# gMLP's v projection by seven products of halves, with its weight sums made on GpSimd in an earlier stage

## Chip, core and metric

One core of a Trainium2 chip runs one program. The metric is the time of one execution in device microseconds (us); the time before is the median of three runs.

## What is computed

The reference runs two transformer blocks over 512 tokens of width 1024, in float32. The change touches the gMLP branch of the first block:

```python
h = rms_norm(x, g_pre_mix)
z = h @ w_in                                  # u, v, q, kv, ... are column ranges of z
y_a = gmlp_mixer(gelu(u), gelu(v), ...)       # u * (W_s LayerNorm(v) + b), in chunks of 128 tokens
merged = g0 * (y_a @ w_br_a) + g1 * (y_b @ w_br_b) + g2 * (y_c @ w_br_c)
```

So v = h @ w_v is a product of 512x1024 by 1024x1024. v is passed through GELU, normalised per token over its 1024 columns, and then mixed over the tokens of a chunk.

## The kernel before

**How a product is computed.** Every large float32 operand is held as two float32r tiles, hi and lo (`split`, L144 and L145: ScalarE rounds hi, VectorE subtracts to get lo), and a product is three matmuls, hi.hi, hi.lo and lo.hi (`mm3`, L129). `load_w` (L188) brings a 512 KB weight tile from HBM on SyncE's queue (SP) into one of two raw buffers (tag `wr`; in `strided_v` there are four more) and splits it into `wh` and `wl`. There are four of these pairs, and with the pool `wx` every fifth pair has a buffer of its own. The instructions of `load_w` have a priority 50 instructions ahead of their place.

**What sets the order.** TensorE works through one stream that is written out by hand. `mm` adds the cost of each matmul to a virtual clock (0.216 for 512 columns), and side tasks (`spawn`, `tick`, `wait`) are generators that yield a delay on that clock; when it has passed, their next instructions are put into the program. `wait()` without arguments empties the list of tasks, however late they are due.

**Stages of the first block.** `nsa_v` (to 37 us of the span), then the compression stage of `nsa` (pool `cmp`, 37 to 97 us): five products of `w_kvc`, of which four are followed by `fold`, which has GpSimd clear a strip of the tile `R` (L1413) and SP copy `R` into `K2` (L1418); between them and after them come three gate products of `w_mg` and twice `hidden`, where four weight tiles of `nsa_wk1` or `nsa_wv1` are used up by 48 matmuls of 256 columns. Then `cmp` is closed and the pool `nsa` is opened in its place, with the tiles `K` and `Q` first. The attention runs to about 405 us, with GpSimd scaling half of the probabilities (L1546). `rnn` follows, and at 579 us `gmlp`.

**gmlp (L765).** `T_` computes v: for each half of the 1024 columns eight k-steps, four token tiles, three matmuls, 192 of 128x128 by 512 columns, from eight weight tiles. As a half of a token tile is done, `done` applies GELU (`gelu`, L434 to L438) and `bn_stats` (L782); after the second half the tile `vg[t]` is normalised (L787). Then, for each of eight column tiles c: product with `w_u`, GELU, product with `w_br_c` (`br_add`), and a task `mixed` that 12.0 (c = 0) or 4.0 clock units after its spawn multiplies all four `vg` with `wT`, scales, adds and splits into `ya` (L807, L810, L145).

**What exists already.** `TS_` (L311) computes a product of 512x1024 by 1024x1024 by Strassen's scheme over halves: seven products of 256x512 by 512x512, each of 24 matmuls of 512 columns, from 14 weight tiles. Three of the seven use the operand itself; four use sums of its quarters. Eight of the 14 weight tiles are sums of quarters of the weight, read from a DRAM tensor that `weight_sums` (L366) made earlier: in four rounds it loads four tiles of 128x512 (L372), GpSimd makes four subtractions (L375 to L378), and four tiles are stored (L381), the transfers on SP's queue. `strided_v` (L1068) uses `TS_` in both layers of the second block; it builds the operand sums on GpSimd and VectorE (L1078 to L1086). Its weight sums are made by `all_weight_sums`, once from `ffn` (817 to 950 us) and once beside the gate products of the second block's first layer (1687 to 1740 us).

Of the kernel before, what the change touches and what calls it, by code (L numbers as in the profile page):

```python
# [50 lines left out]
class Block:  # L51
# [136 lines left out]
    def load_w(self, src, into=None):  # L188
        with self.tc.high_priority(offset=50):
            self.nr += 1  # L190
            rp, n = (self.rawp, 4) if self.rawp and self.nr % 3 else (self.wp, 2)
            raw = rp.tile([P, 1024], F32, tag="wr", name=self.nm("wr"), bufs=n)
            self.nc.sync.dma_start(out=raw, in_=src)
            if into is not None:
                self.split(*into, raw)
                return into
            self.nw += 1
            wp, n = (self.wx, 1) if self.wx and self.nw % 5 == 0 else (self.wp, 4)
            wh = wp.tile([P, 1024], F32R, tag="wh", name=self.nm("wh"), bufs=n)
            wl = wp.tile([P, 1024], F32R, tag="wl", name=self.nm("wl"), bufs=n)  # L200
            self.split(wh, wl, raw)
        return wh, wl
# [161 lines left out]
    def weight_sums(self, src, dst, pool, pace):  # L364

        g = self.nc.gpsimd  # L366
        for i in range(2):
            for o in (slice(0, 512), slice(512, D)):
                q = []
                for half, c in ((0, i), (1, i), (1, 2 + i), (0, 2 + i)):  # L370
                    q.append(pool.tile([P, 512], F32, tag=f"q{len(q)}", name=self.nm("q"), bufs=1))
                    self.nc.sync.dma_start(out=q[-1], in_=src[half][c][:, o])  # L372
                yield pace[0]
# [6 lines left out]
                for j, t in enumerate((b11, b22, b12, b21)):  # L380
                    self.nc.sync.dma_start(out=dst[2 * j + i][:, o], in_=t)  # L381
                yield pace[2]
# [95 lines left out]
    def block1(self):  # L478
# [10 lines left out]
        self.nw, self.wx = 0, None  # L489
        self.nr, self.rawp = 0, None  # L490
        self.wp = op(self.es, "w")
# [48 lines left out]
        with tc.tile_pool(name="gmlp", bufs=1, side="right", reuse_waits="tile") as gp:  # L540
            ya = self.new_op(self.yp, "y", bufs=2)
            mT = self.gmlp(gp, ya, yc)
        es_m.close()
# [220 lines left out]

    def gmlp(self, gp, ya, yc):  # L765
        nc, A, v = self.nc, self.A, self.nc.vector
# [10 lines left out]

        def done(half):
            def f(t, ps):
                o = slice(half * 512, half * 512 + 512)  # L780
                self.gelu(ps, gp, out=vg[t][:, o])
                v.bn_stats(st[t][:, half, :], vg[t][:, o])  # L782
                if half:
                    mv = self.sm(2)
                    v.bn_aggr(mv, st[t])
                    r = self.rsqrt(mv[:, 1:2])
                    v.tensor_scalar(vg[t], vg[t], mv[:, 0:1], r, op0=ALU.subtract, op1=ALU.mult)  # L787
            return f

        for half in range(2):  # L790
            self.T_(self.tok(self.hT), A["w_v"][half], 8, done(half), outer=2 + 2 * half)

# [5 lines left out]
        def mixed(c, gu):  # L798
            yield 12.0 if c == 0 else 4.0
            ps = self.pst()  # L800
# [25 lines left out]
    def ffn(self, hf, fp, es_w):  # L826
# [5 lines left out]
        def done(i, ps):  # L832
            if i == 0:
                self.wait()
                es_w.close()
                pool.append(es.enter_context(tc.tile_pool(name="ffnt", bufs=1, side="right", reuse_waits="tile")))
                self.ada_init(pool[0])
                self.spawn(self.ada(pool[0], 1.9))
                self.w_sums = {}
                self.spawn(self.all_weight_sums(0, pool[0], (12.0, 16.0, 12.0)))  # L840
# [534 lines left out]
    def nsa(self):  # L1375
# [27 lines left out]
        with tc.tile_pool(name="cmp", bufs=1, side="right", reuse_waits="tile") as cp:  # L1403
# [3 lines left out]
            nc.sync.dma_start(out=wv2, in_=A["nsa_wv2"])  # L1407
            k2s = []

            def fold(ps):  # L1410
# [369 lines left out]
```

## Time and profile before

| | |
|---|---|
| median of three runs | 2506.12 us (2503.55 to 2507.12) |
| the profiled execution's own time | 2504.22 us |
| its span, first to last instruction | 2502.2 us |
| TensorE (PE) busy | 2479.7 us, 99% |
| VectorE (DVE) busy | 1457.6 us, 58% |
| ScalarE (ACT) busy | 1072.2 us, 43% |
| GpSimd (POOL) busy | 176.6 us, 7% |
| HBM read and written | 273.86 MB and 21.00 MB |
| granted TensorE clock, mean | 0.999 |

Busy time does not count the issuing of transfers. Matmuls overlap: a matmul of 512 columns lasts 0.39 us, and the next one starts before it has ended. So the cost of one is read from the distance between starts, and a loss is a stretch in which PE's busy time is shorter than the stretch.

### The profile page before, as it was taken

Reading aid. Unit: us, or ns where it says so; the run is one execution under the profiler, and the core shown is the slowest. Engines: PE = TensorE matmul, PEld = TensorE weight load, DVE = VectorE, ACT = ScalarE, POOL = GpSimd, SP = SyncE. Lnnn points to the kernel's source line nnn. Section 1 sums busy time; section 2 is a strip of 40 time slices with the busy share of each in tenths; the row PEclk is TensorE's granted clock in tenths of the full one; section 3 lists DMA queues with packets and bytes.
Section 4 is the critical chain, followed back from the end, with each engine's and each line's share of the span. In section 5 each row is a group of like instructions: output and inputs, shape, how many; then the busy total and the mean of one; then the engine's idle time right before and its main releaser. Section 6 shows DMA issues by size and latency. Waiting matters only on the chain.

```text
span 2502.2 us, 31293 instructions
## 1 busy us (share of the span) xinstructions
PE 2479.7 (99%) x11784; PEld 2044.0 (82%) x11784; DVE 1457.6 (58%) x2701; ACT 1072.2 (43%) x1834; POOL 176.6 (7%) x152
## 2 busy tenths in 40 slices
PE   9999999999999999999999999999999999999998
PEld 7877777888888888888888788888888888888887
DVE  6567665776656788326633536764484343375635
ACT  4477766875334323224444532333253344223323
POOL 0023332000000110001100000003020000000000
PEclk9999999999999999999999999999999999999999
DMA  5522222223345797334432222226444222222233
GB/s 180 171 84 79 68 74 93 94 91 105 118 133 173 264 309 257 127 131 152 161 112 84 65 91 78 91 80 223 143 171 154 89 84 67 94 76 93 68 101 118
DMA packets 110216, 309.54 MB, mean 124 GB/s; under 512 B 14553, under 2 KB 20569, under 8 KB 109938
## 3 DMA queue, kind: packets, MB, share of 16 engines
q1 hardware_dynamic: 109344, 306.31, 37.8%
q8 instruction: 92, 1.51, 0.2%
q10 hardware_dynamic: 722, 1.25, 0.1%
q14 instruction: 58, 0.48, 0.1%
HBM read 273.86 MB, written 21.00 MB: 118 GB/s over the span
## 4 chain that ended last, share of the span: by engine, by line
PE 89%; DVE 4%; ACT 3%; DMA 2%; issue 1%; POOL 0%; ACTq 0%; DVEq 0%; POOLq 0%
PE ps L129 86%; PE ps L138 3%; DVE wl L145 1%; DMA wr<-in_w_out_dram 1%; ACT S L1539 1%; ACT wh L144 1%; DMA wr<-in_w_o_dram 0%; DVE H L145 0%; DVE yr L145 0%; POOL S L1546 0%; ACT S L1544 0%; DVE PTl L145 0%; DVE S L1533 0%; DMA wr<-in_w_mg_dram 0%; POOL X L1084 0%
## 5 line engine op out<-in xcount | busy, mean ns | idle before, releaser
L129 PE MATMUL ps<-h,wh 128*128 128x512 f32 (+1 forms) x4000 | 1243.4, 390 | 0.0
L129 PEld LDWEIGHTS ps<-h,wh 128*128 128x128 f32 x4000 | 734.2, 188 | 139.8 <-issue 5.1
L145 DVE TENSOR_TENSOR wl<-wr,wh 128x1024 fp32r<-128x1024 f32 x395 | 491.2, 1246 | 491.4 <-ACT wh L144 490.6
L129 PE MATMUL ps<-h,wl 128*128 128x512 f32 (+1 forms) x2000 | 772.9, 386 | 0.0
L144 ACT ACTIVATE wh<-wr 128x1024 fp32r<-128x1024 f32 x395 | 417.4, 1059 | 793.5 <-PE ps L129 563.4
L129 PEld LDWEIGHTS ps<-h,wl 128*128 128x128 f32 x2000 | 375.9, 188 | 75.3 <-DVE wl L145 0.4
L129 PE MATMUL ps<-wh,h 128*128 128x512 f32 x672 | 212.5, 393 | 0.2 <-ACT h L144 0.2
L129 PEld LDWEIGHTS ps<-wh,h 128*128 128x128 f32 x672 | 126.9, 189 | 27.5 <-DVE h L145 0.8
L129 PE MATMUL ps<-wl,h 128*128 128x512 f32 x336 | 131.8, 392 | 0.9 <-DVE wl L145 0.9
L129 PE MATMUL ps<-y,wh 128*128 128x512 f32 x384 | 119.2, 391 | 0.0
L665 DVE SCALAR_TENSOR_TENSOR acc<-aw,cact,acc 128x512 f32<-128x512 f32 x96 | 77.7, 810 | 21.2 <-DMA aw<-in_w_ada_dram 19.2
L129 PE MATMUL ps<-wh,f 128*128 128x512 f32 x288 | 89.6, 389 | 0.0
L1546 POOL TENSOR_SCALAR S<-S,sm 128x128 f32<-128x128 f32 (+3 forms) x64 | 69.6, 1099 | 212.4 <-ACT Q L144 87.4
L129 PEld LDWEIGHTS ps<-y,wh 128*128 128x128 f32 x384 | 71.5, 188 | 14.3
L375 POOL TENSOR_TENSOR q<-q,q 128x512 f32<-128x512 f32 x8 | 12.4, 1550 | 983.1 <-PE ps L138 487.6
L129 PE MATMUL ps<-yr,wh 128*128 128x512 f32 x256 | 78.8, 389 | 0.0
L145 DVE TENSOR_TENSOR PTl<-ps,PTh 128x512 fp32r<-128x512 f32 (+1 forms) x96 | 65.1, 684 | 22.5 <-ACT PTh L144 21.6
L1539 ACT ACTIVATE S<-S,sm 128x128 f32<-128x128 f32 (+3 forms) x128 | 70.2, 550 | 18.5 <-DVE sm L1537 18.4
L144 ACT ACTIVATE PTh<-ps 128x512 fp32r<-128x512 f32 (+1 forms) x96 | 56.1, 588 | 48.9 <-PE ps L138 43.9
L1138 DVE CUSTOM_DVE_ANT_0 P<-ps,c_masks 128x128 f32<-128x128 f32 (+1 forms) x96 | 31.1, 324 | 76.5 <-PE ps L129 59.5
L129 PEld LDWEIGHTS ps<-wl,h 128*128 128x128 f32 x336 | 63.6, 189 | 14.7 <-DVE wl L145 1.7
L129 PE MATMUL ps<-y,wl 128*128 128x512 f32 x192 | 74.7, 389 | 0.0
(363 smaller groups left out, 3293.6 us busy)
## 6 DMA issues: line engine op xcount, KB each, us to landing
aw<-in_w_ada_dram SPq DMA_DIRECT2D x96, 256.0 KB, 4.8
wr<-in_w_qk_dram SPq DMA_DIRECT2D x48, 512.0 KB, 3.5
wr<-in_w_ffn_in_dram SPq DMA_DIRECT2D x44, 512.0 KB, 4.5
wr<-in_w_g_dram SPq DMA_DIRECT2D x32, 512.0 KB, 3.5
wr<-in_w_qr_dram SPq DMA_DIRECT2D x32, 512.0 KB, 3.5
wr<-in_w_mg_dram SPq DMA_DIRECT2D x24, 512.0 KB, 3.8
wr<-in_w_ffn_out_dram SPq DMA_DIRECT2D x22, 512.0 KB, 3.4
wr<-in_w_va_dram SPq DMA_DIRECT2D x20, 512.0 KB, 4.6
```

What stands on the lines that cost most here:

```text
L129: self.nc.tensor.matmul(out, a, b, start=start, stop=stop, skip_group_check=True)
L138: self.nc.tensor.transpose(out, in_, self.ident[:k, :k])
L144: nc.scalar.activation(hi, src, AF.Copy)
L145: nc.vector.tensor_sub(lo, src, hi.bitcast(F32))
L375: g.tensor_sub(b11, b12, b11)
L665: v.scalar_tensor_tensor(acc, w, self.cact[:, k:k + 1], acc, op0=ALU.mult, op1=ALU.add)
L1138: v.tensor_tensor_reduce(dst, pv, mask, 1.0, -3e38, ALU.add, ALU.max, mx[:, n:n + 1])
L1539: nc.scalar.activation(Ps[h], Ps[h], AF.Exp, scale=0.125, bias=nm_[:, h:h + 1], accum_out=ls[:, h:h + 1])
L1546: nc.gpsimd.tensor_scalar(Ps[h], Ps[h], r[:, h:h + 1], None, op0=ALU.mult)
```

## The change

`gmlp` computes v with `TS_` in place of two calls of `T_`. The operand sums are made in the four `vg` tiles (two quarters of h on GpSimd, two on VectorE, then three sums on VectorE and one on GpSimd), and three of them are split at once. The fourth is split by a task 14.0 clock units later. The results pass through two `yt` tiles and the second halves of `vg`. While `TS_` runs, two in four raw weight tiles go into the `wx` buffers, which then hold no split weights. `mixed` comes 23.0 clock units after its spawn for c = 0, 11.0 for c = 1, and 4.0 after that as before. `ya` is allocated after `TS_`. The weight sums of v are made by a task in the compression stage, spawned 6.0 clock units into it, with delays of 3.0, 6.5 and 2.5; its four tiles `q` lie in the pool `cmp`. In `weight_sums` GpSimd issues all transfers, also for the two calls that exist already.

```diff
@@ load_w
-            rp, n = (self.rawp, 4) if self.rawp and self.nr % 3 else (self.wp, 2)
-            raw = rp.tile([P, 1024], F32, tag="wr", name=self.nm("wr"), bufs=n)
+            rp, n, tag = (self.rawp, 4, "wr") if self.rawp and self.nr % 3 else (self.wp, 2, "wr")
+            if self.raws_in_wx and self.nr % 4 > 1:
+                rp, n, tag = self.wx, 1, "wh" if self.nr % 4 == 2 else "wl"
+            raw = rp.tile([P, 1024], F32, tag=tag, name=self.nm("wr"), bufs=n)
...
-            wp, n = (self.wx, 1) if self.wx and self.nw % 5 == 0 else (self.wp, 4)
+            wp, n = (self.wx, 1) if self.wx and not self.raws_in_wx and self.nw % 5 == 0 else (self.wp, 4)
@@ weight_sums
-                    self.nc.sync.dma_start(out=q[-1], in_=src[half][c][:, o])
+                    g.dma_start(out=q[-1], in_=src[half][c][:, o])
...
-                    self.nc.sync.dma_start(out=dst[2 * j + i][:, o], in_=t)
+                    g.dma_start(out=dst[2 * j + i][:, o], in_=t)
@@ block1
-            ya = self.new_op(self.yp, "y", bufs=2)
-            mT = self.gmlp(gp, ya, yc)
+            mT = self.gmlp(gp, yc)
@@ gmlp
-        for half in range(2):
-            self.T_(self.tok(self.hT), A["w_v"][half], 8, done(half), outer=2 + 2 * half)
+        hs = self.new_op(self.yp, "y", bufs=2)
+        flat = lambda x, j: x[:, 2 * j:2 * j + 2, :].rearrange("p k q -> p (k q)")
+        a12, a21, a11, a22 = vg
+        for x, kh, th in ((a21, 0, 1), (a22, 1, 1), (a11, 0, 0), (a12, 1, 0)):
+            part = (slice(None), slice(4 * kh, 4 * kh + 4), slice(256 * th, 256 * th + 256))
+            (v if th else nc.gpsimd).tensor_add(x.rearrange("p (k q) -> p k q", k=4), self.hT.hi[part].bitcast(F32),
+                                                self.hT.lo[part].bitcast(F32))
+        v.tensor_add(a22, a21, a22)
+        v.tensor_sub(a21, a11, a21)
+        v.tensor_sub(a11, a22, a11)
+        nc.gpsimd.tensor_sub(a12, a12, a11)
+        for j, x in ((1, a11), (0, a22), (2, a21)):
+            self.split(flat(hs.hi, j), flat(hs.lo, j), x)
+        def fourth():
+            yield 14.0
+            self.split(flat(hs.hi, 3), flat(hs.lo, 3), a12)
+        self.spawn(fourth())
+        places = iter([gp.tile([P, S], F32, tag="yt", name=self.nm("e"), bufs=2) for _ in range(2)]
+                      + [vg[t][:, 512:] for t in range(4)])
+        self.raws_in_wx = True
+        self.TS_(self.hT, [A["w_v"][i] for i in range(2)], self.w_sums["v", 0],
+                 lambda j, k, t, lo: flat(hs.lo if lo else hs.hi, j)[:, k * 256 + t * P:k * 256 + t * P + P],
+                 lambda: next(places), done)
+        self.raws_in_wx = False
+        ya = self.new_op(self.yp, "y", bufs=2)
...
-            yield 12.0 if c == 0 else 4.0
+            yield (23.0, 11.0)[c] if c < 2 else 4.0
@@ nsa, at the start of the compression stage
+            self.w_sums["v", 0] = self.dp.tile([8, P, D], F32, tag="v0", name="v0")
+            self.spawn(self.weight_sums([A["w_v"][i] for i in range(2)], self.w_sums["v", 0], cp, (3.0, 6.5, 2.5)), 6.0)
```

## Rows read from the trace of the kernel before

**Rows 1.** The profile page: busy time by engine, and the chain that ended last by engine.

```profile
PE 2479.7 (99%) x11784; PEld 2044.0 (82%) x11784; DVE 1457.6 (58%) x2701; ACT 1072.2 (43%) x1834; POOL 176.6 (7%) x152
PE 89%; DVE 4%; ACT 3%; DMA 2%; issue 1%; POOL 0%; ACTq 0%; DVEq 0%; POOLq 0%
```

**Rows 2.** Busy time by stretch (us, engines, PEclk, share of the DMA engines, GB/s).

```profile
37.00:97.00 60.00, 58.18 (x309) 48.88 (x308) 34.11 (x41) 28.11 (x37) 0.25 (x2) 1.00 0.63 180
540.00:579.00 39.00, 38.07 (x165) 30.47 (x164) 28.30 (x38) 27.75 (x35) 0.00 (x0) 1.00 0.33 104
579.00:622.70 43.70, 43.70 (x194) 36.21 (x193) 28.21 (x53) 20.91 (x30) 0.00 (x0) 1.00 0.29 90
622.70:653.40 30.70, 30.70 (x143) 25.32 (x143) 24.31 (x51) 13.69 (x19) 0.00 (x0) 1.00 0.46 144
817.00:1000.00 183.00, 183.00 (x891) 154.66 (x891) 150.89 (x190) 59.50 (x78) 22.83 (x16) 1.00 0.83 279
1197.00:1213.50 16.50, 16.07 (x71) 12.96 (x70) 16.50 (x17) 11.86 (x18) 4.11 (x3) 1.00 0.50 161
1680.00:1740.00 60.00, 60.00 (x293) 50.39 (x292) 31.31 (x54) 17.71 (x26) 24.77 (x16) 1.00 0.65 214
```

**Rows 3.** Groups of PE's instructions, 579 to 623.3 us.

```profile
L129 PE MATMUL ps<-wh,h 128*128 128x512 f32 x128 | 39.6, 389 | 0.0
L129 PE MATMUL ps<-wl,h 128*128 128x512 f32 x64 | 24.9, 389 | 0.0
```

**Rows 4.** PE's timeline: the first and the last matmul of v.

```profile
579.25 0.39 PE L129 MATMUL ps<-wh,h 128*128 128x512 f32 x1
...
622.54 0.40 PE L129 MATMUL ps<-wh,h 128*128 128x512 f32 x1
```

**Rows 5.** The tile X of strided_v (ns min/median/max, first and last start).

```profile
L1078 POOL TENSOR_TENSOR X<-h,h x8: 1277/1684/2275, 1171.8 to 1841.9; 128x512 f32<-128x512 f32 x8
...
L359 DVE TENSOR_TENSOR X<-X,ps x4: 678/680/680, 1218.8 to 1882.5; 128x512 f32<-128x512 f32 x4
```

**Rows 6.** Groups of VectorE's instructions, 579 to 650 us.

```profile
L145 DVE TENSOR_TENSOR wl<-wr,wh 128x1024 fp32r<-128x1024 f32 x13 | 15.9, 1223 | 10.6 <-ACT wh L144 10.4
...
L807 DVE SCALAR_TENSOR_TENSOR yt<-ps,c_gmlp_ln,ct 128x512 f32<-128x512 f32 x2 | 1.5, 752 | 0.4 <-PE ps L129 0.2
```

**Rows 7.** The chain of waits, 60 to 130 us (start, length, what).

```profile
72.34 3.35 DMA wr<-in_nsa_wv_dram
...
84.16 4.31 DMA wr<-in_w_mg_dram
...
90.92 4.18 DMA wr<-in_w_q_dram
```

**Rows 8.** DMA issues of the whole run: size, median us to landing.

```profile
wr<-in_w_ffn_in_dram SPq DMA_DIRECT2D x44, 512.0 KB, 4.5
...
q<-in_w_va_dram SPq DMA_DIRECT2D x32, 256.0 KB, 4.8
va<-q SPq DMA_DIRECT2D x32, 256.0 KB, 4.2
...
wr<-in_nsa_wv_dram SPq DMA_DIRECT2D x4, 512.0 KB, 3.9
```

**Rows 9.** The tensor va, SP's transfers (ns, first and last start).

```profile
L381 SPq DMA_DIRECT2D va<-q x32: 319/383/1518, 838.9 to 1736.0; - x32
L193 SPq DMA_DIRECT2D wr<-va x16: 319/319/430, 1183.4 to 1872.5; - x16
```

**Rows 10.** SP's timeline, one round of the weight sums and the next one's start.

```profile
1686.95 1.88 SPq L372 DMA_DIRECT2D q<-in_w_va_dram  x4
...
1696.80 2.16 SPq L381 DMA_DIRECT2D va<-q  x2
1699.05 0.88 SPq L372 DMA_DIRECT2D q<-in_w_va_dram  x2
```

**Rows 11.** The tile Q, 100 to 130 us.

```profile
L144 ACT ACTIVATE Q<-ps x5: 592/592/595, 110.8 to 129.5; 64x512 fp32r<-64x512 f32 x5
```

More of the change, by code (lines that the diff above doesn't have):

```diff
@@ L489, in block1 @@
         self.nw, self.wx = 0, None
-        self.nr, self.rawp = 0, None
+        self.nr, self.rawp, self.raws_in_wx, self.w_sums = 0, None, False, {}
         self.wp = op(self.es, "w")
@@ L762, in rnn, with gmlp @@
         fill()
-    def gmlp(self, gp, ya, yc):
+    def gmlp(self, gp, yc):
         nc, A, v = self.nc, self.A, self.nc.vector
@@ L776, in gmlp @@
         st = [self.smp.tile([P, 2, 6], F32, tag="bn", name=self.nm("bn"), bufs=6) for _ in range(4)]
[L778 to L788, printed above, removed]
@@ L790, in gmlp, with done @@
-        for half in range(2):
-            self.T_(self.tok(self.hT), A["w_v"][half], 8, done(half), outer=2 + 2 * half)
+        def done(t, half, z):
+            o = slice(half * 512, half * 512 + 512)
+            self.gelu(z, gp, out=vg[t][:, o])
+            v.bn_stats(st[t][:, half, :], vg[t][:, o])
+            if half:
+                mv = self.sm(2)
+                v.bn_aggr(mv, st[t])
+                r = self.rsqrt(mv[:, 1:2])
+                v.tensor_scalar(vg[t], vg[t], mv[:, 0:1], r, op0=ALU.subtract, op1=ALU.mult)
@@ L838, in done @@
                 self.spawn(self.ada(pool[0], 1.9))
-                self.w_sums = {}
                 self.spawn(self.all_weight_sums(0, pool[0], (12.0, 16.0, 12.0)))
```

## The prediction

> **What bounds the kernel.** I read the page first. PE is busy for 2479.7 of 2502.2 us, and the chain that ended last is 89% PE [rows 1]. So time is won by matmuls that are not issued, and lost where PE has to wait for an operand. The busy time by stretch shows how much room a stage has [rows 2]. In the v stage PE is busy for all of 43.70 us while VectorE works for 28.21. In the 30.7 us after it PE again waits for nothing. The compression stage is otherwise: PE is busy for 58.18 of 60.00 us, so 1.8 us are lost already, and the DMA engines are busy 0.63 of the time.
>
> **What the seven products remove.** The v stage has 128 + 64 = 192 matmuls of 512 columns [rows 3]. Their first starts at 579.25 and their last at 622.54 [rows 4]: 43.29 us over 191 steps, 0.2266 us each. Seven products of 24 make 168. So 24 are gone, **-5.4 us**, and v ends near 617.3. That is 0.22% of the run, so the gain counts as measurable only if nearly nothing is given back: a measurement of this kernel can tell about 0.2% (5.0 us) from no change.
>
> **Operand sums at the start: covered, but tightly.** The first three products use h itself, so the first sum is due 72 x 0.2266 = 16.3 us after 579, at 595.3. Its chain is one GpSimd addition of 128x1024, at most 2 x 2.28 = 4.6 us by the 128x512 additions of `strided_v` [rows 5], two sums on VectorE, a rounding on ScalarE and a subtraction on VectorE at about 1.22 each [rows 6]: 9.5 us. Three weight subtractions among them make 13.2, under 16.3. VectorE also stood idle for 10.7 of the 39.0 us before 579 [rows 2], and only the fourth operand has to wait for the recurrent branch's last tiles, so part of this can come earlier. The fourth operand's split is due only in the seventh product; that it is 14 units later costs nothing, since the second product lies over it. The nearest row for the whole start is the same scheme in `strided_v`, where VectorE was busy for all of 16.50 us and PE lost 0.43 [rows 2]. I take **+0.4**.
>
> **VectorE over the whole stage.** VectorE gets 6 more weight subtractions (7.3 us by 1.22 each), 5 operand sums and 4 low parts (9 x 1.22 = 11.0) [rows 6], and 12 additions out of PSUM at 0.68 (8.2) [rows 5]: 26.5 us. `mixed` for c = 0 is spawned near 623.7 (617.3, the row sums' matmul and one product of 5.4) and comes 23 units, 24.1 us, later: at 648. By then VectorE owes what it did before up to 648 + 5.4 = 653.4, which is 28.21 + 24.3 = 52.5 [rows 2], plus 26.5, less the two mixings that were moved out (three passes near 0.75 each, 4.5) [rows 6]: 74.5 us in 69. With at most 10.7 us done ahead it is 64 to 75: VectorE is full for all that time. Ends: nothing, as residual additions and GELUs of u can slip behind; and 74.5 - 69 = 5.5 us if PE must wait at the mixing for all of it. The nearest row is again the full stretch, 0.43 lost in 16.5 us; I take two more of these, **+0.9**. Moving the mixing costs PE nothing by itself: the work is the same, and `w_u` and `w_br_c` products fill the place. Fourteen weight tiles in 38 us are a demand that `strided_v` meets with six raw buffers; here two `wx` tiles make it four, and the fifth split pair is lost for that time. I price that inside the same term.
>
> **The weight sums in the compression stage.** 32 transfers of 256 KB are 8.4 MB, beside the 180 GB/s x 60 us = 10.8 MB that the stage moves [rows 2]: about 320 GB/s, more than the 279 at which the engines were busy 0.83 of the time from 817 to 1000. There PE lost nothing, but there a weight tile lasts 24 matmuls, 5.4 us; in `hidden` four tiles go in as long (48 matmuls of half the width). In the chain of waits this stage hangs on weight transfers: three pieces of 3.35, 4.31 and 4.18 us stand on it [rows 7]. So what lengthens them lengthens the run. In the stage with the other weight sums a 512 KB tile landed in 4.5 us, against 3.9 for `nsa_wv` here [rows 8]: 3 x 0.6 = **+1.8**. Ends: nothing, if the rounds miss those three; and if each takes what a `q` load half its size took there, twice 4.8 at most, 3 x (9.6 - 3.9) = 17, which I do not believe as a whole, since two queues share and neither stops; half of it, 8.5, is my upper end. In this term I also put GpSimd's clearing of `R`, which now queues behind subtractions that wait for their loads, with SP's `K2` copies and the weight transfers behind them waiting for it.
>
> **GpSimd as the issuer of the older weight sums.** Their 64 transfers leave SP. PE lost nothing in either stage (183.00 of 183 and 60.00 of 60), and GpSimd was busy for 22.83 and 24.77 us of them [rows 2], so there is neither a gain to fetch nor a lack of room. The last sum was stored at 1736.0 and the second set first read after 1842, where the sums for that `strided_v` begin [rows 5, 9]: 100 us of cover. **0.**
>
> **Sum.** -5.4 + 0.4 + 0.9 + 1.8 = -2.3 us. The profiled execution took 2504.22 us; the median of the runs is 1.9 above it. On the median: 2506.1 - 2.3 = 2503.8.
>
> **Rivals.**
>
> *Nothing is given back* (0.30). VectorE does the sums in the holes before 579, the weight tiles are ahead, the rounds miss the critical transfers. For it: 10.7 idle us, the zero loss from 817 to 1000. Against: the chain through three weight transfers. 2506.1 - 5.4 = 2500.7, with up to 0.6 less if the small gaps at the end of v vanish: 2500 to 2501.
>
> *The sums end too late and hold up the attention: slower* (0.15). The tiles `q` lie in `cmp`, and the pool `nsa`, with `K` and `Q` first, takes that place. A round took 12.1 us from its first load to the next one's when SP issued (1686.95 to 1699.05) [rows 10]. Four rounds from 43 us, with 4.2 for the last store [rows 8], end near 96; `Q` is first written at 110.8 [rows 11]. The margin is 15 us. No row shows a transfer issued by GpSimd; SP takes 0.4 to 0.5 us for one of these [rows 10]. The point from which this decides is 15 / 32 = 0.46 us more per issue. With 0.75 us more the sums end 24 us late, and ScalarE, which writes `Q` and rounds the weights in one queue, waits 9 us: 2503.8 + 9 = 2513. By the Trainium skill (DMA: Bandwidth & Descriptors, "Latency and other measured facts") a transfer of GpSimd's path has its first byte after about 1 us against 0.6 on the others; by that estimate the sums would be 13 us later and end just ahead of `Q`, and the time would stay 2503.8. The Trainium skill (SBUF — State Buffer, "SBUF: two separate sides") speaks against this change: GpSimd writes the descriptors itself and is locked out while VectorE runs in a two-port mode; no row of before can show that, as SP issued everything.
>
> *The weight transfers of the compression stage give all of it back: slower* (0.10). Upper end of that term: 2506.1 - 5.4 + 1.3 + 8.5 = 2510.5. Against: SP's queue and GpSimd's share the engines, and 0.63 is not full.
>
> *VectorE is the new bound after v.* Upper end of that term, 5.5 us: 2506.1 - 5.4 + 0.4 + 5.5 + 1.8 = 2508.4, which counts as the same. It stands within the forecast.
>
> **How the numbers follow.** The forecast, a gain partly given back, has 0.45, and gives "same" (2501.1 to 2511.1). The clean gain gives faster, 0.30; the two slower ones 0.25. The range is from 2499.0 (all gained, runs a little low) to 2511.5; beyond it are late sums above 8 us, and little else. The forecast's own range is 2501 to 2508.5.
>
> **What would show it.** Right: 168 matmuls of v in about 38 us, PE's loss in that stretch under 1 us, VectorE near full from 579 to 648, a compression stage some 2 us longer than 60 us. Wrong on the start: PE waiting for the tile `y` after the third product. Wrong on VectorE: PE waiting for `vg` at the first mixing, or for `wl`. Wrong on the sums: GpSimd's last store after 110, and ScalarE's write of `Q` waiting for it. Wrong altogether: a stretch outside 37 to 130 and 579 to 717 that changed by over 2 us.

## The result, and the profile after

The changed kernel takes 2521.53 us (median of 6 runs, 2516.18 to 2523.00), the kernel before 2505.35 (6 runs): a ratio of 1.0061, 95% interval 1.0050 to 1.0072. It is 16 us slower where 2 us less were forecast, and outside the range. The profiled execution took 2522.35 us, its span 2520.6; it is 18.1 us over the profiled execution before, while the medians are 16.2 apart.

The profile page of the changed kernel, busy time by engine and the chain by engine:

```profile
PE 2483.3 (99%) x11760; PEld 2043.9 (81%) x11760; DVE 1494.1 (59%) x2728; ACT 1083.8 (43%) x1846; POOL 260.3 (10%) x267
...
PE 83%; DVE 7%; DMA 3%; ACT 3%; issue 2%; POOL 1%; SPq 0%; ACTq 0%; DVEq 0%; POOLq 0%
```

Against [rows 1] PE has the 24 matmuls fewer that were promised (11784 to 11760), and yet the chain hangs less on PE (83% for 89%) and more on VectorE (7% for 4%) and the DMA (3% for 2%). GpSimd's busy time contains the issuing of its own transfers: from 37 to 111 us it makes 8.2 of the changed kernel's 18.54. Where the time went is read from when the same matmul of PE comes in the two traces. Each column below is the start of one matmul, in us behind the kernel before (in the kernel before itself: the time from the span's start). The kernels of the later rows are the experiments. Each row is one execution, and f2b_half_subs stands at -1.5 in the first column with nothing changed before it: differences of 1 to 2 us say little by themselves.

| | first of the compression stage | first of the attention | last of the attention | last gate of `rnn` | row sums, right after v | last mixing | last of all |
|---|---|---|---|---|---|---|---|
| before, at | 36.9 | 122.9 | 404.4 | 564.1 | 622.8 | 717.1 | 2494.9 |
| after | +4.2 | +14.4 | +15.5 | +15.6 | +13.4 | +17.5 | +18.3 |
| e1_unused | +2.6 | +11.5 | +12.6 | +12.7 | +12.7 | +12.7 | +13.7 |
| e2_raw | -0.7 | -0.4 | +0.1 | +0.1 | -2.1 | -0.1 | -0.1 |
| e3_va_pool | -0.6 | -0.7 | +0.1 | +0.6 | +0.6 | +0.6 | +0.3 |
| f1_transfers | +3.3 | +4.1 | +5.2 | +5.2 | +5.2 | +5.2 | +6.3 |
| f3_clear_dve | +2.9 | +11.2 | +11.6 | +11.6 | +11.6 | +11.6 | +12.9 |
| f4_held | -0.2 | +11.1 | +11.7 | +11.9 | +11.9 | +11.9 | +10.9 |
| f5_half_transfers | -0.1 | +5.5 | +5.8 | +5.8 | +5.8 | +5.8 | +6.5 |
| f2b_half_subs | -1.5 | +2.4 | +3.4 | +3.4 | +3.4 | +3.4 | +5.2 |
| f6_half_both | -1.0 | +6.7 | +7.7 | +7.7 | +7.7 | +7.7 | +9.6 |
| g2_fourth_dve | -1.2 | -0.9 | -1.2 | -1.4 | -5.0 | -3.2 | -2.1 |
| g3_mix_later | -0.9 | -0.5 | -0.7 | -0.8 | -4.4 | -4.4 | -2.6 |
| k1_after_mix | +4.3 | +14.4 | +14.9 | +14.8 | +11.2 | +11.2 | +10.7 |
| k3_sp_issue | -0.3 | +14.7 | +15.2 | +15.1 | +14.0 | +15.3 | +15.8 |
| e4_rnn | -0.1 | +0.3 | +1.1 | +24.7 | +21.2 | +26.1 | +26.3 |
| h1_rnn_late | -0.4 | -0.1 | -0.4 | +6.9 | +4.7 (see there) | +8.7 | +8.6 |
| h3_att_pool | -0.1 | +0.1 | +6.3 | +6.3 | +2.7 | +2.7 | +4.3 |
| h3_att_sp | -0.3 | +0.2 | +2.4 | +2.9 | -0.7 | -0.7 | -1.0 |

So the changed kernel loses 4.2 us before the compression stage, 10.2 in it and 1.1 in the attention. It wins 2.2 in v and loses 4.1 by the end of the mixing. Busy time by stretch (PE, PEld, DVE, ACT, POOL, then the granted clock, the DMA engines' share, GB/s). First come two stretches of the kernel before that [rows 2] lack:

```profile
10.00:20.00 10.00, 9.75 (x42) 7.31 (x42) 8.55 (x19) 7.25 (x14) 0.00 (x0) 1.00 0.55 161
37.00:111.00 74.00, 72.18 (x376) 60.50 (x375) 40.12 (x48) 34.05 (x45) 0.25 (x2) 1.00 0.62 180
```

Then the changed kernel:

```profile
10.00:20.00 10.00, 7.56 (x21) 5.35 (x22) 8.22 (x14) 5.19 (x10) 8.34 (x10) 1.00 0.93 300
37.00:111.00 74.00, 65.99 (x319) 54.51 (x317) 42.95 (x50) 29.76 (x38) 18.54 (x25) 0.95 0.68 199
595.00:634.00 39.00, 36.92 (x160) 29.46 (x159) 34.68 (x40) 23.04 (x28) 6.64 (x1) 1.00 0.53 173
634.00:665.00 31.00, 31.00 (x136) 25.05 (x134) 29.80 (x69) 19.17 (x29) 0.00 (x0) 1.00 0.48 150
665.00:735.00 70.00, 67.74 (x324) 57.15 (x324) 47.35 (x78) 27.25 (x40) 0.00 (x0) 0.98 0.36 109
817.00:1000.00 183.00, 183.00 (x934) 156.64 (x933) 160.39 (x213) 61.63 (x88) 40.36 (x48) 1.00 0.83 282
1700.00:1760.00 60.00, 60.00 (x290) 50.30 (x289) 32.18 (x55) 18.59 (x26) 37.84 (x45) 1.00 0.62 212
```

**The start.** From 10 to 20 us the DMA engines are busy 0.93 in place of 0.55, and PE issues 21 matmuls in place of 42. GpSimd's timeline shows whose transfers these are (start, length, line, output<-input, and the idle time before it with what ended it):

```profile
1.28 2.28 POOL L374 DMA_DIRECT2D q<-in_w_v_dram  x4 [0.43 <-issue]
...
9.25 1.26 POOL L377 TENSOR_TENSOR q<-q,q 128x512 f32<-128x512 f32 x1 [5.55 <-DMA q<-in_w_v_dram]
...
33.67 0.54 POOL L374 DMA_DIRECT2D q<-in_w_v_dram  x1 [0.19 <-issue]
55.96 0.12 POOL L1439 MEMSET R<- 128x32 f32 x1 [21.75 <-DMA K<-R]
56.44 1.60 POOL L374 DMA_DIRECT2D q<-in_w_v_dram  x3 [0.36 <-issue]
...
81.64 1.09 POOL L383 DMA_DIRECT2D v<-q  x2
```

The task is spawned in the compression stage, but nothing in GpSimd's queue is ahead of it. So the first four loads leave at 1.28 us, beside the first weights that PE needs. After two rounds the clearing of `R` stands in the same queue and waits 21.75 us for its buffer. That puts rounds three and four at 56 to 83 us, on the hidden products.

**The compression stage.** The chain that ended last, in that stage (start, length, what), and what PE waited for from 37 to 111 us (total, times, longest):

```profile
47.80 5.75 DMA wr<-in_w_mg_dram
...
62.73 6.39 DMA wr<-in_nsa_wk_dram
...
72.71 6.76 DMA K<-R
...
82.02 1.20 DVE wl L145
...
85.56 4.42 DMA wr<-in_nsa_wv_dram
```

```profile
PE ps L129 <- DVE wl L145: 3.7, 3, 2.3
PE ps L138 <- ACT g L1449: 1.9, 1, 1.9
...
```

The stage hangs on weight transfers as it did in [rows 7], only now on longer ones, and on `K2` copies that did not stand on the chain before. VectorE is late as well. Its subtractions for `wl` and additions for `blk` in the same 74 us, before and then the additions after (busy, mean ns of one, idle before):

```profile
L145 DVE TENSOR_TENSOR wl<-wr,wh 128x1024 fp32r<-128x1024 f32 x20 | 24.4, 1224 | 24.2 <-ACT wh L144 24.2
L1439 DVE TENSOR_TENSOR blk<-K,pe 128x256 f32<-128x256 f32 x16 | 8.7, 603 | 4.8 <-DMA K<-R 4.8
```

```profile
L1465 DVE TENSOR_TENSOR blk<-K,pe 128x256 f32<-128x256 f32 x16 | 13.1, 865 | 10.0 <-DMA K<-R 10.0
```

The additions take 865 ns in place of 603, and wait 10.0 us for their copies in place of 4.8. The granted clock adds to it. After the stall near 72 us it is 0.57 for 4 us, which is 1.2 in place of 2.4 GHz for most of that stretch, and full again after. The same comes behind the stall at the first mixing products, where 0.62 over 4.5 us is worth about 0.38 x 4.5 = 1.7 us:

```profile
71.00:73.50 2.50, 1.15 (x7) 1.06 (x8) 2.50 (x4) 1.63 (x3) 0.76 (x2) 1.00 0.77 219
73.50:77.50 4.00, 4.00 (x12) 3.09 (x11) 1.42 (x3) 0.00 (x0) 2.13 (x3) 0.57 0.99 262
77.50:81.00 3.50, 3.50 (x28) 3.24 (x26) 2.16 (x2) 0.43 (x1) 3.40 (x4) 1.00 0.65 208
...
664.00:667.00 3.00, 1.09 (x5) 0.56 (x3) 3.00 (x8) 1.31 (x3) 0.00 (x0) 1.00 0.14 19
667.00:671.50 4.50, 4.15 (x13) 3.51 (x14) 4.33 (x13) 2.91 (x5) 0.00 (x0) 0.62 0.49 148
```

**v and the mixing.** v's 168 matmuls start over 41.0 us (594.92 to 635.92), against 43.29 for 192 in [rows 4]; at 0.2266 each, 167 steps would be 37.8. GpSimd's group with the fourth operand sum, what ScalarE then waited for, and what PE waited for from 660 to 670 us:

```profile
L800 POOL TENSOR_TENSOR vg<-vg,vg 128x1024 f32<-128x1024 f32 x1 | 6.6, 6642 | 19.2 <-DVE vg L799 19.2
```

```profile
ACT y L144 <- POOL vg L800: 5.4, 1, 5.4
```

```profile
PE ps L129 <- DVE sm L156: 2.3, 1, 2.3
```

One subtraction of 128x1024 takes GpSimd 6.64 us, where its two additions of that size before v took 2.6 each. ScalarE, which rounds the weights in the same queue, stands for 5.4 us waiting for it. Later PE waits 2.3 us at the first mixing products for VectorE's normalisation of `vg` (`sm` at L156 belongs to its reciprocal root; the chain's last piece before the products is `vg`, L787).

### The profile page after: what moved, and what is told of

Its sections match the earlier page's. It is cut to its first block, busy times and chain, and to the rows that moved or that the text cites. A ratio compares the mean times of both kernels' runs of the same rounds, so it can differ in the third digit from the quotient of the medians.

```text
span 2520.6 us, 31410 instructions
## 1 busy us (share of the span) xinstructions
PE 2483.3 (99%) x11760; PEld 2043.9 (81%) x11760; DVE 1494.1 (59%) x2728; ACT 1083.8 (43%) x1846; POOL 260.3 (10%) x267
## 4 chain that ended last, share of the span: by engine, by line
PE 83%; DVE 7%; DMA 3%; ACT 3%; issue 2%; POOL 1%; SPq 0%; ACTq 0%; DVEq 0%; POOLq 0%
PE ps L129 81%; PE ps L138 3%; DVE wl L145 2%; DMA wr<-in_w_out_dram 1%; ACT wh L144 1%; ACT S L1565 1%; DMA wr<-in_w_o_dram 0%; DMA wr<-in_w_mg_dram 0%; DMA K<-R 0%; DVE H L145 0%; DMA wr<-in_w_v_dram 0%; DVE yr L145 0%; POOL vg L800 0%; DVE y L145 0%; DMA wr<-in_nsa_wk_dram 0%
## 5 line engine op out<-in xcount | busy, mean ns | idle before, releaser
L145 DVE TENSOR_TENSOR wl<-wr,wh 128x1024 fp32r<-128x1024 f32 x401 | 502.0, 1255 | 483.7 <-ACT wh L144 482.5
L144 ACT ACTIVATE wh<-wr 128x1024 fp32r<-128x1024 f32 x401 | 423.4, 1058 | 783.7 <-PE ps L129 546.7
L129 PE MATMUL ps<-wh,h 128*128 128x512 f32 x592 | 188.4, 395 | 2.0 <-ACT h L144 2.0
L129 PEld LDWEIGHTS ps<-wh,h 128*128 128x128 f32 x592 | 112.0, 190 | 26.3 <-ACT h L144 2.6
L129 PE MATMUL ps<-wl,h 128*128 128x512 f32 x296 | 116.7, 394 | 1.6 <-DVE wl L145 1.6
L374 POOL DMA_DIRECT2D q<-in_w_va_dram x32 | 17.3, 543 | 715.0 <-DVE mv L1338 482.6
L129 PEld LDWEIGHTS ps<-wl,h 128*128 128x128 f32 x296 | 56.1, 190 | 14.5 <-DVE wl L145 3.2
```

Source lines behind the costliest of these rows:

```text
L129: self.nc.tensor.matmul(out, a, b, start=start, stop=stop, skip_group_check=True)
L144: nc.scalar.activation(hi, src, AF.Copy)
L145: nc.vector.tensor_sub(lo, src, hi.bitcast(F32))
L374: g.dma_start(out=q[-1], in_=src[half][c][:, o])
```

## Experiments

Every ratio is against runs of the kernel before on the same chip.

**e1_unused: the weight sums alone.** The kernel before, with v's weight sums added as the change has them (GpSimd issues these; the older sums stay on SP). Nothing reads them.

```diff
...
 k2s = []
+vs = self.dp.tile([8, P, D], F32, tag="v0", name="v0")
+self.spawn(self.weight_sums([A["w_v"][i] for i in range(2)], vs, cp, (3.0, 6.5, 2.5), nc.gpsimd), 6.0)
```

> The kernel before, with v's weight sums made in the compression stage on GpSimd as in the change, but used by nobody; the older weight sums stay on SP. Theory A (the loss is made by where the sums are computed: in the changed trace the attention's first K.Q matmul came 14.4 us and its last 15.6 us later): 2505.3 + 14 to 16 = 2519 to 2521. Rival B (the early delay is mostly taken back in the attention and the loss sits in the new gmlp): under 2510.

Measured: 2519.07, ratio 1.0056 (1.0041 to 1.0071). The sums alone cost nearly the whole loss, 2.6 us ahead of the stage and 8.9 in it.

**e2_raw: the new gmlp alone.** The changed kernel without v's weight sums; plain quarters of the weight stand in their place, so v is not the reference's.

```diff
-self.TS_(self.hT, [A["w_v"][i] for i in range(2)], self.w_sums["v", 0],
+self.TS_(self.hT, [A["w_v"][i] for i in range(2)], [A["w_v"][i][c] for i in range(2) for c in range(4)],
...
-self.spawn(self.weight_sums([A["w_v"][i] for i in range(2)], self.w_sums["v", 0], cp, (3.0, 6.5, 2.5)), 6.0)
```

> The changed kernel without v's weight sums: the five products with summed weights read plain quarters of w_v instead, so v is not the reference's; operand sums, 14 weight tiles, 168 matmuls and the mixing are as in the change. Theory A: what is left is the gain of 5.4 us less some 7 us lost in gmlp (in the changed trace the delay went from 15.6 us before v to 13.4 after it and 17.6 after the mixing): 2505.3 + 1 to 3 = 2506 to 2508. Rival B: over 2515.

Measured: 2504.28, ratio 1.0000 (0.9991 to 1.0009). Better than expected, but the 5.4 us are gone: v gains 2.2 and the mixing loses 2.0.

**e3_va_pool: the issuer alone.** The kernel before, with the older sums' transfers on GpSimd.

```diff
-self.nc.sync.dma_start(out=q[-1], in_=src[half][c][:, o])
+g.dma_start(out=q[-1], in_=src[half][c][:, o])
...
-self.nc.sync.dma_start(out=dst[2 * j + i][:, o], in_=t)
+g.dma_start(out=dst[2 * j + i][:, o], in_=t)
```

> The kernel before, with only the issuer changed: GpSimd issues the transfers of the two older weight sums. Both theories: no change, 2504 to 2507. If the issuer costs by itself (the changed trace gained 0.9 us of delay around the start of the feed-forward stage), 2506 to 2508.

Measured: 2504.85, ratio 1.0001 (0.9991 to 1.0010): no cost, as forecast.

**f1_transfers, f3_clear_dve, f4_held: where in the sums.** All three are e1_unused with one edit: v's four subtractions left out; VectorE clears `R` in place of GpSimd; the first round held until the last token's h is written.

```diff
# f1
-g.tensor_sub(b11, b12, b11)
...
# f3
-nc.gpsimd.memset(R[:, 512:544], 0.0)
+v.memset(R[:, 512:544], 0.0)
# f4
+if eng is g and i == 0 and o.start == 0:
+    g.tensor_copy(q[-1][:, :1], self.hT.hi[:, 7, S - 1:S].bitcast(F32))
 eng.dma_start(out=q[-1], in_=src[half][c][:, o])
```

> As e1_unused (the kernel before, with unused sums of w_v; 2519.1), but without the 16 subtractions: each round loads four tiles and stores them as they are. Theory A1 (the transfers take the weight tiles' share of the DMA engines, and the stages to 125 us hang on weight tiles): most of the 14.9 us stays, 2514 to 2519. Rival A2 (GpSimd's subtractions hold VectorE's instructions up): under 2509.

Measured: 2510.21, ratio 1.0021 (1.0012 to 1.0030), between both expectations. It tells little, since without subtractions the transfers run ahead: they delay the start by 3.3 us and the stage by only 0.8.

> As e1_unused, but VectorE clears the strip of R, so that neither the clearing waits behind the sums on GpSimd nor the sums behind a clearing that waits for R's buffer (in e1_unused the third round stood from 36 to 57 us for that, and the last two rounds fell on the two hidden products). Theory A1 alone: the same bytes, 2516 to 2520. Rival A3 (GpSimd's one queue is what costs): 2508 to 2513.

Measured: 2516.09, ratio 1.0046 (1.0031 to 1.0061). That is 11.5 us over its chip's kernel before, where e1_unused was 14.9 over: GpSimd's long wait in front of `R` (21.75 us in the changed kernel) is worth some 3 us, and the two intervals overlap.

> As e1_unused, but the first round's tiles are first touched by a copy of one column of the last token's h, so no transfer of the sums can be issued before about 25 us (in e1_unused the first four are issued at 1.3 to 3.1 us, among the loads of x and of the first weights, and the first F product starts 2.6 us later). Theory A: the 2.6 us at the start go, and the rounds fall on the compression stage instead, which loses as much or more: 2516 to 2522. Rival (the start is an independent loss and the later rounds cost the same): 2515 to 2517.

Measured: 2518.11, ratio 1.0054 (1.0039 to 1.0069). The delay at the start is gone (-0.2), and the stage takes it over: +11.3 in it. Holding the sums back moves the loss and does not lessen it.

**f5_half_transfers, f2b_half_subs, f6_half_both: transfers against subtractions.** The kernel before with two of the four rounds, both held until the third and fourth `R` are written, so that all of it falls in the compression stage. f5 leaves out v's subtractions, f2b the transfers, f6 neither.

```diff
-for i in range(2):
+for i in range(1, 2):
...
+while len(self.Rs) < 3 + r: yield 0.5
+g.tensor_copy(q[-1][:, :1], self.Rs[2 + r][:, :1])
# f5
-g.tensor_sub(b11, b12, b11)
...
# f2b
-eng.dma_start(out=q[-1], in_=src[half][c][:, o])
+g.memset(q[-1][:, :], 1.0)
...
-eng.dma_start(out=dst[2 * j + i][:, o], in_=t)
```

> The kernel before, with only half of v's weight sums issued by GpSimd and nothing using them, held back until the third and fourth folded weight exist, so that they fall inside the compression stage; here with their 8 loads and 8 stores (of 256 KB each) but without the subtractions. All four rounds inside that stage cost about 11 us, so two should cost about 5.5 when whole. Theory A1 (the loss is the compression stage's own weight loads coming late behind the added transfers): 2508 to 2511. Theory A2 (the loss is VectorE slowed by GpSimd's subtractions): within 1 us of the kernel before, 2504 to 2506.

> As the run with transfers only, but the other way round: the same 8 subtractions of 128x512 on GpSimd at the same place (their operands filled by GpSimd itself), no transfer at all. A1 (late weight loads): 2504 to 2506. A2 (VectorE slowed by GpSimd): 2507 to 2510.

> The same half of the sums whole, transfers and subtractions. Both theories: 2508 to 2511, that is about half of what the four rounds cost in this stage; if the two costs add, it is the sum of the other two runs' differences, and if it is much more, each is harmless alone and the order of the stage decides.

Measured: 2510.19 (ratio 1.0021, 1.0011 to 1.0031), 2509.44 (1.0017, 1.0007 to 1.0026) and 2512.36 (1.0031, 1.0019 to 1.0042), against 2504.49. So transfers cost 5.7 us, subtractions 5.0, both 7.9 (f6 is above its 2508 to 2511). Neither theory holds alone: each part is enough for a loss. Busy time from 37 to 111 us, PE's longest wait and the longest transfer on the chain that ended last, of f5:

```profile
37.00:111.00 74.00, 67.61 (x351) 57.09 (x350) 38.83 (x46) 32.80 (x43) 12.67 (x26) 0.98 0.73 223
```

```profile
PE ps L129 <- ACT hidT L1478: 3.9, 1, 3.9
```

```profile
80.52 7.37 DMA wr<-in_nsa_wv_dram
```

of f2b, with VectorE's groups:

```profile
37.00:111.00 74.00, 69.95 (x358) 58.71 (x357) 45.96 (x46) 32.37 (x42) 20.81 (x22) 0.98 0.59 172
```

```profile
L145 DVE TENSOR_TENSOR wl<-wr,wh 128x1024 fp32r<-128x1024 f32 x19 | 26.1, 1378 | 16.6 <-ACT wh L144 16.6
L1453 DVE TENSOR_TENSOR blk<-K,pe 128x256 f32<-128x256 f32 x16 | 10.6, 713 | 4.8 <-DMA K<-R 4.8
```

In f5 VectorE works no longer than before (38.83 against 40.12 us), the DMA engines are at 0.73 in place of 0.62, and one load of `nsa_wv` holds the chain for 7.37 us, where that of [rows 7] held it for 3.35. In f2b the DMA share is no higher than before (0.59), but VectorE is busy for 5.8 us more with two instructions fewer: `wl` takes 1378 ns against 1224 in the kernel before, `blk` 713 against 603. The four clears of `q` per round are work that the change does not have, so I take 5.0 as an upper bound for these subtractions; in the table 3.9 of it lies in the stage. The Trainium skill (SBUF — State Buffer, "Who interferes with whom") says that a VectorE instruction with two SBUF inputs contends with a GpSimd instruction that reads SBUF. The trace agrees: both groups have two such inputs.

**g2_fourth_dve and g3_mix_later: the rest of gmlp.** e2_raw with the fourth operand on VectorE (g2), and with the mixing put off as well (g3). v is not the reference's in either.

```diff
-nc.gpsimd.tensor_sub(a12, a12, a11)
+v.tensor_sub(a12, a12, a11)
# g3 also
-yield (23.0, 11.0)[c] if c < 2 else 4.0
+yield (29.0, 17.0, 6.0)[c] if c < 3 else 4.0
```

> As e2_raw (the new gmlp without sums of the weight, plain quarters in their place, v not the reference's; 2504.3), but VectorE makes the fourth operand's last subtraction, which took GpSimd 6.65 us in the changed trace and held up ScalarE's queue for 5.4 us, with 2.2 us of PE waiting behind it. If that wait is the loss: 2501.5 to 2502.5. If VectorE as a whole is what binds (it then has 1.2 us more to do): 2504 to 2505.5.

Measured: 2503.00, ratio 0.9997 (0.9987 to 1.0007), between both expectations.

> The changed kernel without weight sums and with the fourth operand's subtraction back on VectorE (2503.0), and with the mixing products of the first three channel blocks put off further (29, 17 and 6 clock units in place of 23, 11 and 4). Theory M1 (what v's saving still loses is TensorE waiting for the mixing's VectorE operands, issued too early for them): 2500 to 2502, and no wait of 2 us at the first mixing products. Theory M2 (VectorE is full from the start of v to the end of the mixing, so the time that v saves is waited out somewhere before the end of it): 2502.5 to 2504.

Measured: 2500.83, ratio 0.9986 (0.9977 to 0.9996), 3.7 us below the kernel before. v's matmuls now start over 39.6 us in both, 3.7 less than before, and in g3 the mixing costs nothing more. What PE waited for from 579 to 735 us, in e2_raw and then in g3:

```profile
PE ps L129 <- DVE sm L156: 1.6, 1, 1.6
PE ps L129 <- ACT wh L144: 1.1, 1, 1.1
...
```

```profile
PE ps L129 <- DVE wl L145: 1.5, 1, 1.5
```

Of the 5.4 us a wait of 1.5 for `wl` within v remains.

**k1_after_mix: do the pieces add?** The changed kernel whole, with the two edits of g3.

> The changed kernel whole, with two edits behind the sums: the fourth operand's subtraction on VectorE in place of GpSimd, and the first mixing products put off further (29, 17, 6 clock units). If the loss consists of separate pieces, v's and the mixing's share of 5.4 minus 0 comes back and the rest stays: 2521.5 - 3.7 = about 2518 (2516 to 2519.5). If the late compression stage hides or feeds the later loss, so that the pieces don't add, it is 2520 or more, or under 2515.

Measured: 2513.14, ratio 1.0037 (1.0023 to 1.0051). It is 9.1 us over its chip's kernel before, and the changed kernel was 16.2 over: 7.1 come back, where the same edits gave 3.8 without sums (e2_raw to g3). That is under the 2515 at which the pieces don't add; but the intervals of the four ratios are wider than this difference, so that it is not shown by the medians. In the table 1.4 come back in v, as without sums, and 4.1 in the mixing, which in e2_raw cost 2.0. The wait there was 2.3 us in the changed kernel and 1.6 in e2_raw, and in these two executions the granted clock fell behind the first alone (0.62 above, 1.00 in e2_raw's stretch from 634 to 665). The rest, some 2 us from the last mixing to the end and in the attention, I can't place; single executions differ by as much.

**k3_sp_issue: GpSimd's queue or the place?** The changed kernel, all weight sums' transfers back on SP (the diff of e3_va_pool, reversed).

> The changed kernel, with one part undone: all weight sums' transfers are issued by SyncE, as in the kernel before; the sums of v stay in the compression stage. SyncE issues in a written order, behind the first weight loads, so the first four transfers can't come at 1.3 us. Theory B1 (the place of the sums is what costs, not the queue that issues them): the start delay of 4 us goes, the rounds fall inside the stage instead, 2517 to 2523. Theory B2 (it is GpSimd's queue, by its early start and its waits, that costs): under 2512.

Measured: 2519.21, ratio 1.0058 (1.0043 to 1.0073). The start is undisturbed (-0.3), the compression stage loses 15.0. So in this stage the issuer decides only where the loss falls, and the sums cost as much either way.

**e4_rnn and h1_rnn_late: the recurrent stage.** The changed kernel with the sums in `rnn`, in the two `wx` buffers. h1 differs from e4 in the pace (4, 6 and 1 clock units against 6, 9 and 5) and in that raw weights of v never go there, so that v has two raw buffers in place of four; it has the edits of g3 as well.

```diff
...
# e4
+self.spawn(self.weight_sums_wx([A["w_v"][i] for i in range(2)], self.w_sums["v", 0], (6.0, 9.0, 5.0), nc.gpsimd), 6.0)
# h1
+self.spawn(self.weight_sums_wx([A["w_v"][i] for i in range(2)], self.w_sums["v", 0], (4.0, 6.0, 1.0), nc.gpsimd), 6.0)
-if self.raws_in_wx and self.nr % 4 > 1:
+if self.raws_in_wx and self.nr > self.late and self.nr % 4 > 1:
```

> The changed kernel with v's weight sums moved from the compression stage into the recurrent stage (405 to 579 us), GpSimd issuing, the four tiles in the wx buffers, paces 6.0, 9.0, 5.0. Theory A: as without the sums at all, 2506 to 2509, since the DMA engines are busy 0.3 there and weight tiles last 5.4 us. Rival C (16 subtractions and 32 transfers cost the same wherever they run): 2515 or more.

Measured: 2530.33, ratio 1.0096 (1.0079 to 1.0113): a miss by over 20 us. What SP's queue waited for from 404 to 580 us, and SP's timeline near 491 us:

```profile
SPq L195 <- DMA v<-q: 27.9, 4, 19.8
```

```profile
490.91 0.33 SPq L195 DMA_DIRECT2D wr<-in_w_v_dram  x1
491.34 0.40 SPq L195 DMA_DIRECT2D wr<-in_w_br_b_dram  x1
```

A raw weight of v, due much later, had been put ahead of a weight that the stage needs (`w_br_b`), and waited there for the sums' stores.

> The changed kernel with v's sums in the recurrent stage, in the buffers of two spare weights, issued by GpSimd (as in the run at 2530.3), but with no raw weight of v in those two buffers, so that SyncE's queue has no load that waits for the sums' stores ahead of the loads that the stage needs; with the fourth operand's subtraction on VectorE and the mixing put off, as in the run without sums at 2500.8. Theory C1 (the 26 us lost there came from SyncE's queue held by those loads; transfers and subtractions are covered in that stage, whose DMA share was 0.29 to 0.35): 2500 to 2504, below the kernel before. Theory C2 (the subtractions lengthen VectorE's work there as they did in the compression stage, where it was less busy): 2508 or more.

Measured: 2515.18, ratio 1.0043 (1.0028 to 1.0058): most of that is gone, but 7.3 us are still lost in the stage. How much the pace did of it and how much the buffers is not separated. In v nothing is won: its matmuls start over 45.4 us, the last 12 of them behind the row sums, so that v's end is at +8.8 and not at the +4.7 of the table's column; the mixing adds nothing to that. From 440 to 500 us, before and in h1, and `wl` in h1 from 440 to 510:

```profile
440.00:500.00 60.00, 60.00 (x265) 49.42 (x264) 46.60 (x72) 51.44 (x71) 0.00 (x0) 1.00 0.30 97
```

```profile
440.00:500.00 60.00, 53.67 (x226) 42.85 (x224) 57.89 (x65) 43.30 (x60) 39.12 (x42) 0.97 0.59 199
```

```profile
L145 DVE TENSOR_TENSOR wl<-wr,wh 128x1024 fp32r<-128x1024 f32 x9 | 14.0, 1567 | 0.0
```

The DMA has room (0.59). VectorE has hardly any: it is busy for 57.89 of 60 us with seven instructions fewer, and `wl` takes 1567 ns, where it took 1220 in the kernel before. That this is what costs here fits theory C2; no run of this stage leaves out the subtractions alone.

**h3_att_pool and h3_att_sp: the attention, without GpSimd's subtractions.** The changed kernel with the edits of g3 and the sums in the attention stage, in buffers of `K` and of `HL` that stand free late in it; VectorE subtracts. The first lets GpSimd issue, the second SP.

```diff
...
+q = [pool.tile([P, S], F32R, tag=t, name=self.nm("q"), bufs=b).bitcast(F32) for t, b in (("K", 10), ("K", 10), ("HL", 2), ("HL", 2))]
...
-g.tensor_sub(b11, b12, b11)
+v.tensor_sub(b11, b12, b11)
...
-(qproj, 6), (qproj, 7)]
+(qproj, 6), (qproj, 7), (sums, 0)]
```

> The changed kernel with the sums of v in the attention stage (282 us long, VectorE 0.68 and the DMA 0.26 busy there in the kernel before), in four buffers that stand free once the last queries are projected; the subtractions by VectorE in place of GpSimd (16 of about 0.7 us, 11 us in all), the transfers issued by GpSimd; with v's fourth operand on VectorE and the mixing put off. Theory D1 (what the sums need is a stage with slack in VectorE and the DMA, and no GpSimd subtraction beside a full VectorE): 2500 to 2503, faster than the kernel before. Theory D2 (GpSimd's queue, which there also scales the scores and adds the outputs, now waits for transfers and VectorE, and attention waits for it): 2506 or more.

Measured: 2507.00, ratio 1.0009 (1.0000 to 1.0019).

> The same, with the sums' transfers issued by SyncE, in whose queue the weight loads stand behind the sums' waits. D1: 2500 to 2503. D3 (SyncE's queue is held by the sums' waits ahead of weight loads, as in the run at 2530.3): 2508 or more. If the GpSimd variant is slow and this one is not, or the other way round, the queue and not the stage decides.

Measured: 2502.82, ratio 0.9992 (0.9982 to 1.0001), 2.4 us below the kernel before (2505.23), which the interval just fails to tell from no change, and clearly below the changed kernel. From 300 to 404 us, before and in h3_att_sp:

```profile
300.00:404.00 104.00, 103.12 (x528) 80.72 (x526) 69.68 (x217) 74.86 (x179) 36.53 (x34) 1.00 0.23 74
```

```profile
300.00:404.00 104.00, 102.32 (x517) 79.30 (x516) 76.80 (x227) 74.15 (x179) 38.05 (x34) 1.00 0.43 144
```

VectorE has room, 76.80 of 104 with the subtractions, and so has the DMA (0.23 before, 0.43 now); the sums cost 2.2 us in the attention. With GpSimd as the issuer they cost 6.2, in the same stage with the same subtractions. GpSimd's queue there also scales the probabilities; it waited 6.6 us in 4 stores for VectorE's subtractions:

```profile
POOL v L401 <- DVE q L397: 6.6, 4, 3.4
```

That this wait makes the difference of 4 us fits, but no run shows it alone. Both runs change the stage and the engine that subtracts at once. No run has VectorE subtract in the compression stage or GpSimd in the attention, so what each of the two gave is not shown.

## Why the prediction was wrong

The step that failed most is the term for the weight sums, +1.8: they cost 14.4 us up to the attention. The terms for the operand sums and VectorE, 1.3 together, were mis-sized as well: 7.3.

*The matmuls removed, -5.4: right.* 24 are gone. With a wait of 1.5 left in v its starts span 3.7 us less (g2, g3), and the whole run is 3.7 us shorter (g3).

*The operand sums and VectorE, +0.4 and +0.9: mis-sized.* v lost 41.0 - 37.8 = 3.2 and the mixing 4.1, 7.3 against 1.3. The sums that are due first came in time: three low parts were done by 609.9, before 594.9 + 16.3 = 611.2. Two other steps failed. "The fourth operand's split ... costs nothing, since the second product lies over it" priced the split and not the subtraction in front of it, which on GpSimd took 6.64 us beside VectorE, against the 4.6 that I gave an addition of that size at most, and held ScalarE's queue. With that subtraction on VectorE v gets back 1.4 (g2). And "moving the mixing costs PE nothing by itself" was wrong by its place: at 23 units VectorE was still behind. Put off by 6 units more, the mixing costs nothing (g3). VectorE's work came out at the lower end of the forecast 64 to 75 us: 34.68 + 29.80 = 64.5 from 595 to 665. So it was not its sum that cost, but what was late at one place; and the half clock behind that wait, some 1.7 us, was in no term.

*The sums in the compression stage, +1.8: the step that failed most.* They cost 4.2 at the start and 10.2 in the stage. Three things in it were wrong. "Four rounds from 43 us" took the place where the task is spawned for the time when its transfers start; GpSimd's queue, empty until then, started them at 1.28. The transfers' own price was small only by its choice of rows. The estimate of 0.6 us for each `nsa_wv` load was right, but the median of `nsa_wk` lengthened by 1.7 and that of the `K2` copies by 1.1, while that of `w_mg` fell from 5.5 to 3.8. Part of this is chance: in e3, whose stage is that of before, `nsa_wk` has 4.9 and `K2` 2.9. On the chain, loads of 5.75, 6.39 and 4.42 us and a copy of 6.76 stand among others where I had counted three loads. The DMA issues from 37 to 111 us of before and then of after, median us to landing at the end of each line:

```profile
K<-R SPq DMA_DIRECT2D x16, 132.0 KB, 3.8
wr<-in_nsa_wk_dram SPq DMA_DIRECT2D x4, 512.0 KB, 4.3
```

```profile
K<-R SPq DMA_DIRECT2D x16, 132.0 KB, 4.9
wr<-in_nsa_wk_dram SPq DMA_DIRECT2D x4, 512.0 KB, 6.0
wr<-in_nsa_wv_dram SPq DMA_DIRECT2D x4, 512.0 KB, 4.5
```

And the term had no price for GpSimd's subtractions beside VectorE, which by themselves cost up to 5.0 us for half of the rounds (f2b). The reassurance from 817 to 1000 us, where PE loses nothing beside sums of the same kind, did not carry over to a stage in which PE already waited for 1.8 us. How the 10.2 us divide among late loads, the slowed VectorE and the clock stays open: f5 and f2b show that transfers and subtractions each cost, with half of the rounds.

*GpSimd as the issuer of the older sums, 0: right* (e3; PE is busy for 183.00 of 183 in the changed kernel too).

*The rivals.* "Nothing is given back" needed sums that cost nothing; no run with sums had that, and h3_att_sp came nearest. "The sums end too late" did not come: the last store is issued near 82, well ahead of the attention. "The weight transfers give all of it back" named the right stage and half of the mechanism, with an upper end of 8.5 us that a chain of late loads, a slowed VectorE, a late start and a lower clock together passed.

*What was to show it.* "A compression stage some 2 us longer" and "wrong altogether: a stretch outside 37 to 130" were the tests that the trace failed: 10.2 us, and 4.2 before 37. PE's wait at the first mixing, the sign of being wrong on VectorE, came as well.

## What to carry to other kernels

Work put on an idle queue starts when its buffers are free, not where its task stands in the program: read the queue's order before pricing it, and give it a dependence if it must wait. Before hanging side work on a stage, ask for room in every resource that it takes, VectorE among them when GpSimd subtracts beside it, and be wary of a stage in which PE already waits. Side work moved to a stage whose DMA engines were busy 0.23 of the time in place of 0.62, with the subtractions taken off GpSimd and SP as the issuer, cost 2 us where it had cost 14; VectorE's share alone would not have told the stages apart, as it was 0.54 in the one that lost and 0.67 in the other.

## What was not expected of the hardware

- A GpSimd subtraction of 128x1024 took 6.64 us (606.63 to 613.27), while its two additions of that size at 582 took 2.6 each. From 606.39 to 611.02 VectorE ran four subtractions of two SBUF inputs back to back, each at its usual 1.22 us; GpSimd's ended 2.2 us after the last of them. In h1 it was VectorE's that stretched: `wl` from 1220 to 1567 ns.
- A wait of PE of 2.3 us at the mixing was followed by 4.5 us at a granted clock of 0.62, one of 1.6 us by none. The length of the wait is not all: in v the changed kernel and k3 both have two gaps, after which the next matmul starts 1.43 and 1.26 us after the one before, and only k3 had the low clock behind them. The changed kernel and then k3:

```profile
616.50:621.00 4.50, 4.38 (x19) 3.65 (x20) 4.50 (x6) 4.47 (x6) 0.00 (x0) 1.00 0.65 207
```

```profile
616.50:621.00 4.50, 4.50 (x14) 3.55 (x13) 4.50 (x6) 4.32 (x6) 0.00 (x0) 0.62 0.66 228
```

- GpSimd took 0.54 to 0.57 us to issue a transfer of 256 KB; SP took 0.44 to 0.47 for a load [rows 10] and 0.38 for a store [rows 9]. Its loads were no later for it: 5.1 us to landing with the older sums on GpSimd (e3) against 4.8 [rows 8], and their stores landed sooner, 3.1 against 4.2.
